# Gate and up of a feed-forward layer: weights stationary against tokens stationary, with the results turned by block transposes and DMAs

## The chip, the cores and the metric

One core of a Trainium2 chip runs the whole kernel. The metric is device time in microseconds (us), the median of several runs. PE is the tensor engine (matmul), PEld its weight load, DVE the vector engine, ACT the scalar engine, POOL the engine for general work, SP the one that issues most DMAs. All arithmetic is in float32; each big product is made of three passes of a split form (below).

## The reference, cut to what matters

Two transformer blocks, 256 tokens (S) by 2048 features (D), batch 1. The first has a sliding-window attention; the second has two attention branches and a gated feed-forward layer. What the change touches is the end of the second block:

```python
h2 = rmsnorm_2(x, ffn_norm_g[i])
x = x + (jax.nn.silu(h2 @ w_ffn_gate[i]) * (h2 @ w_ffn_up[i])) @ w_ffn_down[i]
return rmsnorm_2(x, final_norm_g)
```

`w_ffn_gate` and `w_ffn_up` are 2048 x 5632, `w_ffn_down` is 5632 x 2048.

## The kernel before

**Split form.** A matrix entry is held as hi + lo, hi rounded to the matmul's format and lo the rest. A product is hi x hi + hi x lo + lo x hi. Weights come from HBM in chunks of 16 tiles of 128 x 128 (1 MB, by SP, four buffers); `Weights.cut` (line 60) splits half a chunk (8 tiles) at a time: ACT casts to w_hi (line 84), DVE subtracts to w_lo (line 85). Four halves of each are held, so the splits run up to four halves ahead of PE and then wait for PE to give a buffer back.

**Two forms of product.** `gemm` (line 319) keeps a weight tile stationary and moves the tokens: per tile one 512-column matmul (hi weights against hi and lo of the 256 tokens side by side) and one 256-column matmul (lo weights against hi tokens); `runs` (line 307) does eight of one kind, then eight of the other. Its result has features on partitions and tokens along the row. `gemm_nat` (line 375) with `nat3` (line 367) keeps a 128 x 128 block of tokens stationary and moves four weight tiles (512 columns): hi x hi, hi x lo, lo x hi, for each of two token blocks, so six 512-column matmuls per row of four weight tiles. Its result has tokens on partitions.

**The stage.** After the product `out`, x2 holds the residual and `h` the 16 normed blocks (features on partitions, h3_0 to h3_15). Gate and up are `gemm` products, 44 blocks of 128 columns each: for each block m the gate product, its scaling by the norm's factor (a row broadcast `rb` made by `rows`, line 282, with a matmul), Silu, the up product, the multiply, and a split into `act[m]`, which has features on partitions as the down product needs it. The first four products run together over four banks (`gemm4`, line 329). The down product is `gemm_nat`, tokens stationary; its results are added to x2n, the residual turned to tokens on partitions.

**What sets the order.** `between` (line 126) holds generators of side work. Every product calls `between.tiles`, and after `between.every` weight tiles (16 here) one step of side work is written into the program; `yield n` asks for n such ticks of pause. In this stage the side work is `after_out` (line 940): it makes the norm's factor r_3, the broadcast, and then eight x2n pieces, each from four PE transposes and a copy on ACT. A scheduler orders the instructions of each engine from that program; every engine runs its own list in order. POOL computes the norms' powers (line 279) and issues five DMAs: a table (`lam`) and the four gain tiles `fgt` (line 978). Small tiles come from one pool, `unit`, of 67 buffers of 128 x 512.

Of the kernel before, what the change touches and what calls it, by code (L numbers as in the profile page):

```python
# [9 lines left out]
F32 = mybir.dt.float32  # L10
# [4 lines left out]
P = 128  # L15
S = 256
# [154 lines left out]
def block_kernel(ctx, tc, order, w, x01, xt, bc, fg, cst, out):  # L171
# [10 lines left out]
    def unit(name, dt=F32):  # L182
        return up.tile([P, 512], dt, name=name, tag="u", bufs=NU)
# [4 lines left out]
    def bank(tag):  # L188
        return psum.tile([P, 512], F32, name=f"ps_{tag}", tag=tag, bufs={"g": 4, "s": 2, "t": 2}[tag])
# [92 lines left out]
    def rows(r, rb=None):  # L282

        dg = unit("diag")[:, 0:S]
        for tb in range(2):
            nc.vector.tensor_scalar(out=dg[:, tb * P:tb * P + P], in0=ident, scalar1=r[:, tb:tb + 1], scalar2=None,
                                    op0=ALU.mult)
        ps = bank("t")
        mm(ps[:, 0:S], ones, dg, True, True)
        if rb is not None:  # L290
            nc.vector.tensor_copy(out=rb, in_=ps[:, 0:S])
        return ps[:, 0:S]
# [73 lines left out]

    def nat3(o, hl, tb, hi, lo, first, last):

        xh = hl[:, tb * P:tb * P + P]
        xl = hl[:, S + tb * P:S + tb * P + P]  # L370
        mm(o, xh, hi, first, False)
        mm(o, xh, lo, False, False)
        mm(o, xl, hi, False, last)
# [13 lines left out]
    def total(o, ps):  # L387

        nc.scalar.copy(out=o, in_=ps[:, S:])  # L389
        tt(o, o, ps[:, 0:S], ALU.add)  # L390

    def scaled(o, ps, rb):
        total(o, ps)
        tt(o, o, rb, ALU.mult)
# [24 lines left out]
    def transposed(p, on_act=False):  # L419

        ps = bank("t")
        for j in range(3):
            nc.tensor.transpose(out=ps[:, j * P:j * P + P], in_=p[:, j * P:j * P + P], identity=ident)  # L423
        pt = unit("prob_t")[:, 0:384]
        if on_act:
            nc.scalar.copy(out=pt, in_=ps[:, 0:384])
        else:
            nc.vector.tensor_copy(out=pt, in_=ps[:, 0:384])
        return pt


    sq = Squares(8)
# [493 lines left out]
    for m, ps in blocks("out", 0, 16, mg):  # L926
# [5 lines left out]
        split_scaled(t, gcol(G_FFN, m), hl)  # L932
        h.append(hl)
        sq.add(t)
    rb = unit("rb_3")[:, 0:S]
    r_3 = const.tile([P, 2], F32, name="r_3")
    x2n = []

    def after_out():
        yield  # L940
        nc.vector.tensor_copy(out=r_3, in_=rstd(sq.sums(), D))
        yield
        rows(r_3, rb)
        for cb in range(4):
            for tb in range(2):
                yield
                ps = bank("t")
                for i in range(4):
                    nc.tensor.transpose(out=ps[:, i * P:i * P + P], in_=x2[4 * cb + i][:, tb * P:tb * P + P],  # L949
                                        identity=ident)  # L950
                t = unit("x2n")
                nc.scalar.copy(out=t, in_=ps)
                x2n.append(t)

    between.every, between.apart = 16, 1
    between.add(after_out())
    act = []
    for m in range(0, KF):
        if m == 0:
            b4 = gemm4("ffn", [0, KF, 1, KF + 1], h)  # L960
        t = unit("ffn")
        zg, zu = t[:, 0:S], t[:, S:]
        ps = b4[2 * m] if m < 2 else gemm("ffn", m, h)
        scaled(zg, ps, rb)
        nc.scalar.activation(out=zg, in_=zg, func=AF.Silu)
        ps = b4[2 * m + 1] if m < 2 else gemm("ffn", KF + m, h)
        total(zu, ps)
        tt(zu, zu, zg, ALU.mult)
        hl = unit(f"act{m}", F32R)
        split_scaled(zu, None, hl)  # L970
        act.append(hl)
    between.drain()

    tot = sm("tot", 10)
    fgt = []
# [81 lines left out]
    return c  # L1057


def _columns(v):  # L1060
    return np.asarray(v, np.float32).reshape(-1, P).T


def _matrices(i):

    pairs = []
    for j in range(16):
        kt = j // 8
        for hd in (16 * kt + j % 8, 16 * kt + 8 + j % 8):
            pairs.extend(range(hd * 64, hd * 64 + 64))  # L1070
    pairs = np.array(pairs)
    in_a, in_2 = i["w_in_a"][0], i["w_in_2"][0]
    uq = i["w_uq_2"][0].reshape(768, 16, 192)
    ukv = i["w_ukv_2"][0].reshape(512, 16, 256)
    kpe = in_2[:, 1280:1344]
    ffn = np.concatenate([i["w_ffn_gate_2"][0], i["w_ffn_up_2"][0]], axis=1)
    return {
        "in_a": np.concatenate([in_a[:, :2048][:, pairs], in_a[:, 2048:2560], in_a[:, 2560:][:, pairs]], axis=1),
        "out_a": i["w_out_a"][0][pairs],
        "in_2": in_2[:, :1280],  # L1080
        "kpe": np.concatenate([kpe, kpe], axis=1),
        "dqk": in_2[:, 1344:5440],
        "dv": in_2[:, 5440:7488],
        "gate": in_2[:, 7488:],
        "uq": np.concatenate([uq[:, :, :128].reshape(768, -1), uq[:, :, 128:].reshape(768, -1)], axis=1),
        "uk": ukv[:, :, :128].reshape(512, -1),
        "uv": ukv[:, :, 128:].reshape(512, -1),
        "mla": i["w_mla_proj_2"][0],
        "diff": i["w_diff_proj_2"][0],
        "out": i["w_out_2"][0],  # L1090
        "ffn": ffn,
        "down": i["w_ffn_down_2"][0],
    }


# [32 lines left out]
```

## Time and profile before

| | us |
|---|---|
| median of 3 runs | 2023.06 (2022.99 to 2024.19) |
| profiled execution | 2023.11 |
| its span | 2021.3 |
| gate and up, first matmul to down's first | 494.40 |
| down, first matmul to its last part | 233.69 |

PE is busy 2007.7 us of the span, DVE 1309.4, ACT 1074.6, POOL 18.4; 364.83 MB move by DMA, 180 GB/s on average. The mean granted clock of PE is 0.999 of full speed. A matmul's own duration overlaps the next one's, so a pace is read from one start to the next. A table by stage gives for each engine its busy time and, in brackets, its instructions.

### The profile page before, as it was taken

To read this page: it belongs to the slowest core of one execution; us is meant where nothing else is said; L and a number is where in the kernel's file an instruction comes from. 1 tells how busy PE (TensorE), PEld (TensorE's weight loads), DVE (VectorE), ACT (ScalarE), POOL (GpSimd) and SP (SyncE) were. 2 spreads that over 40 slices of the span, in tenths; PEclk is the share of its full clock that TensorE was granted. 3 is DMA by queue.
4 is the path that set the end of the run, shared out by engine and by line. 5 is a ranking of instruction groups with operands and counts; after the bars stand their busy time and mean duration, and the time that the engine had idled before them with its cause. 6 is when DMAs were issued, how large, how long until landed. Compare 5 with 4: busy or idle time off the path is not lost.

```text
span 2021.3 us, 28390 instructions
## 1 busy us (share of the span) xinstructions
PE 2007.7 (99%) x11338; PEld 1744.3 (86%) x11338; DVE 1309.4 (65%) x2151; ACT 1074.6 (53%) x1821; POOL 18.4 (1%) x25
## 2 busy tenths in 40 slices
PE   9999999999999999999999999999999999999998
PEld 8888888888888888888888888888888888888887
DVE  7778766887857555576665667656666666554544
ACT  6677665756546444455565445554444445444443
POOL 0000000000000000000000000000000000000000
PEclk9999999999999999999999999999999999999999
DMA  8444454444344555545445555455555555555553
GB/s 300 152 144 149 165 209 176 167 149 155 135 169 167 188 188 188 190 167 186 172 166 188 192 196 190 175 179 187 189 188 189 192 191 191 194 209 189 196 197 104
DMA packets 53235, 364.83 MB, mean 180 GB/s; under 512 B 6064, under 2 KB 6576, under 8 KB 9968
## 3 DMA queue, kind: packets, MB, share of 16 engines
q1 hardware_dynamic: 51552, 359.76, 49.8%
q10 hardware_dynamic: 1152, 1.97, 0.3%
q8 instruction: 88, 1.44, 0.3%
q0 software_dynamic: 400, 1.31, 0.2%
q14 instruction: 43, 0.35, 0.1%
HBM read 360.91 MB, written 2.10 MB: 180 GB/s over the span
## 4 chain that ended last, share of the span: by engine, by line
PE 96%; DVE 2%; ACT 1%; issue 1%; DMA 0%; POOL 0%; POOLq 0%; ACTq 0%
PE ps_g L198 88%; PE ps_s L198 5%; PE ps_t L198 2%; PE ps_t L423 1%; DVE rope_t L201 1%; DVE w_lo L85 0%; DVE k_n L201 0%; DVE q_r L201 0%; ACT w_hi L84 0%; DMA x01t<-x 0%; PE ps_t L949 0%; PE ps_t L853 0%; ACT prob L414 0%; PE ps_t L829 0%; DVE prob L408 0%
## 5 line engine op out<-in xcount | busy, mean ns | idle before, releaser
L85 DVE TENSOR_TENSOR w_lo<-w_raw,w_hi 128x1024 fp32r<-128x1024 f32 (+1 forms) x677 | 824.9, 1220 | 296.7 <-ACT w_hi L84 276.3
L84 ACT CAST w_hi<-w_raw 128x1024 fp32r<-128x1024 f32 (+1 forms) x677 | 708.2, 1047 | 352.9 <-PE ps_g L198 269.5
L198 PE MATMUL ps_g<-h,w_hi 128*128 128x512 f32 x3048 | 742.1, 392 | 0.1
L198 PEld LDWEIGHTS ps_g<-h,w_hi 128*128 128x128 f32 x3048 | 558.4, 188 | 111.2 <-issue 3.5
L198 PEld LDWEIGHTS ps_g<-h,w_lo 128*128 128x128 f32 x3048 | 392.1, 191 | 17.8 <-issue 3.2
L198 PE MATMUL ps_g<-h,w_lo 128*128 128x256 f32 x3048 | 404.0, 284 | 0.0
L198 PE MATMUL ps_g<-w_hi,act 128*128 128x512 f32 x688 | 212.1, 389 | 0.0
L198 PEld LDWEIGHTS ps_g<-w_hi,act 128*128 128x128 f32 x688 | 129.1, 188 | 26.9
L389 ACT COPY ffn<-ps_g 128x256 f32<-128x256 f32 x86 | 31.8, 373 | 200.6 <-PE ps_g L198 200.6
L198 PE MATMUL ps_g<-w_lo,act 128*128 128x512 f32 x344 | 133.8, 389 | 0.0
L201 DVE TENSOR_TENSOR ffn<-ffn,ps_g 128x256 f32<-128x256 f32 x86 | 35.8, 420 | 143.9 <-ACT ffn L389 143.9
L198 PE MATMUL ps_g<-w_hi,h 128*128 128x512 f32 x256 | 79.5, 389 | 0.0
L198 PEld LDWEIGHTS ps_g<-w_lo,act 128*128 128x128 f32 x344 | 64.6, 188 | 13.3
L198 PE MATMUL ps_g<-y_m,w_hi 128*128 128x512 f32 x256 | 63.8, 391 | 0.0
L198 PE MATMUL ps_g<-y_d,w_hi 128*128 128x512 f32 x256 | 61.2, 391 | 0.0
L198 PE MATMUL ps_g<-g,w_hi 128*128 128x512 f32 (+1 forms) x240 | 57.8, 377 | 0.0
L198 PEld LDWEIGHTS ps_g<-w_hi,h 128*128 128x128 f32 x256 | 48.0, 188 | 10.0
L198 PE MATMUL ps_g<-mg,w_hi 128*128 128x512 f32 x224 | 56.0, 391 | 0.0
L198 PEld LDWEIGHTS ps_g<-y_m,w_hi 128*128 128x128 f32 x256 | 47.0, 188 | 9.1
L198 PEld LDWEIGHTS ps_g<-y_d,w_hi 128*128 128x128 f32 x256 | 47.0, 188 | 9.1
L198 PE MATMUL ps_g<-c,w_hi 128*128 128x512 f32 x208 | 53.0, 397 | 0.0
L198 PE MATMUL ps_g<-w_lo,h 128*128 128x512 f32 x128 | 49.8, 389 | 0.0
(255 smaller groups left out, 1899.4 us busy)
## 6 DMA issues: line engine op xcount, KB each, us to landing
w_raw<-w SPq DMA_DIRECT2D x337, 1024.0 KB, 4.8
w_raw<-w SPq DMA_DIRECT2D x5, 512.0 KB, 7.6
x_t<-xt SPq DMA_DIRECT2D x7, 256.0 KB, 7.4
fgt<-fg POOLq DMA_DIRECT2D x4, 256.0 KB, 5.5
out<-x2n SPq DMA_DIRECT2D x4, 256.0 KB, 3.1
out<-x2n ACTq DMA_DIRECT2D x4, 256.0 KB, 3.5
x01t<-x SPq DMA_DIRECT2D x1, 310.0 KB, 4.8
w_raw<-w ACTq DMA_DIRECT2D x1, 256.0 KB, 5.0
```

What stands on the lines that cost most here:

```text
L84: a = nc.scalar.copy(out=hi[:, q], in_=src[:, q])
L85: b = nc.vector.tensor_tensor(out=lo[:, q], in0=src[:, q], in1=hi.bitcast(F32)[:, q], op=ALU.subtract)
L198: nc.tensor.matmul(out=o, lhsT=a, rhs=b, start=start, stop=stop, skip_group_check=True)
L201: nc.vector.tensor_tensor(out=o, in0=a, in1=b, op=op)
L389: nc.scalar.copy(out=o, in_=ps[:, S:])
L423: nc.tensor.transpose(out=ps[:, j * P:j * P + P], in_=p[:, j * P:j * P + P], identity=ident)
```

## The change

Gate and up become `gemm_nat` products, 11 groups of four blocks: one gate product of 512 columns, one up product of 512 columns, each for two token blocks. The norm's factor is now a scalar per partition inside Silu, so the broadcast goes (and, as before, the up half is left unscaled until the end). The result has tokens on partitions and has to be turned. DVE transposes 32 x 32 blocks in place within a 128 x 512 tile (`nc.vector.transpose`); then `moved` exchanges the blocks between partition quarters with 16 DMAs of 32 partitions x 128 columns, issued by POOL. `split_act`, added to `between` after each group, waits five ticks and then splits the two pieces into act_hi and act_lo. The x2n pieces are turned the same way, with no PE transposes: the first three ticks after r_3, the others eight ticks apart. The columns of gate, up, down, the final gain and the output are permuted on the host (`_quarters`) so that the blocks come out in place. `between.drain()` ahead of the down product is gone: the last group's split is written inside down's first product.

```diff
     def nat3(o, hl, tb, hi, lo, first, last):
-        xh = hl[:, tb * P:tb * P + P]
-        xl = hl[:, S + tb * P:S + tb * P + P]
+        if isinstance(hl, list):
+            xh, xl = hl[tb]
+        else:
+            ...
+    def moved(tr, name):
+        o = unit(name)
+        for a in range(4):
+            for b in range(4):
+                nc.gpsimd.dma_start(out=o[32 * b:32 * b + 32, a * P:a * P + P],
+                                    in_=tr[32 * a:32 * a + 32, b * P:b * P + P])
+        return o
     def after_out():
         yield
         nc.vector.tensor_copy(out=r_3, in_=rstd(sq.sums(), D))
-        yield
-        rows(r_3, rb)
         for cb in range(4):
             for tb in range(2):
-                yield
-                ps = bank("t")
+                yield 8 if x2n else 3
+                tr = unit("x2_t")
                 for i in range(4):
-                    nc.tensor.transpose(out=ps[:, i * P:i * P + P], in_=x2[4 * cb + i][:, tb * P:tb * P + P],
-                                        identity=ident)
-                t = unit("x2n")
-                nc.scalar.copy(out=t, in_=ps)
-                x2n.append(t)
+                    nc.vector.transpose(
+                        out=tr.rearrange("p (a m j) -> p a m j", a=4, m=4)[:, :, i, :],
+                        in_=x2[4 * cb + i][:, tb * P:tb * P + P].rearrange("p (a j) -> p a j", a=4))
+                x2n.append(moved(tr, "x2n"))
-    for m in range(0, KF):
-        if m == 0:
-            b4 = gemm4("ffn", [0, KF, 1, KF + 1], h)
-        t = unit("ffn")
-        zg, zu = t[:, 0:S], t[:, S:]
-        ps = b4[2 * m] if m < 2 else gemm("ffn", m, h)
-        scaled(zg, ps, rb)
-        nc.scalar.activation(out=zg, in_=zg, func=AF.Silu)
-        ps = b4[2 * m + 1] if m < 2 else gemm("ffn", KF + m, h)
-        total(zu, ps)
-        tt(zu, zu, zg, ALU.mult)
-        hl = unit(f"act{m}", F32R)
-        split_scaled(zu, None, hl)
-        act.append(hl)
-    between.drain()
+    def split_act(u, parts):
+        yield 5
+        hls = []
+        for t in parts:
+            t = t.rearrange("p (a g i) -> p g a i", a=4, g=4)
+            hi, lo = unit("act_hi", F32R), unit("act_lo", F32R)
+            nc.scalar.copy(out=hi.rearrange("p (g a i) -> p g a i", a=4, g=4), in_=t)
+            tt(lo.rearrange("p (g a i) -> p g a i", a=4, g=4), t,
+               hi.bitcast(F32).rearrange("p (g a i) -> p g a i", a=4, g=4), ALU.subtract)
+            hls.append((hi, lo))
+        for k in range(4):
+            q = slice(k * P, k * P + P)
+            act[4 * u + k] = [(hi[:, q], lo[:, q]) for hi, lo in hls]
+    for u in range(KF // 4):
+        parts = []
+        for tb, ps in enumerate(gemm_nat("ffn", u * 512, h)):
+            z = unit("ffn")
+            nc.scalar.activation(out=z, in_=ps, func=AF.Silu, scale=r_3[:, tb:tb + 1])
+            parts.append(z)
+        for tb, ps in enumerate(gemm_nat("ffn", DFF + u * 512, h)):
+            z = parts[tb]
+            tt(z, ps, z, ALU.mult)
+            tr = unit("ffn_t")
+            nc.vector.transpose(out=tr, in_=z)
+            parts[tb] = moved(tr, "ffn_m")
+        between.add(split_act(u, parts))
```

How the instructions stand, at three places. First PE, inside one of the early up products of before: the end of the lo passes of a product (bank ps_g_12681, normed blocks h3), four transposes of residual tiles y into ps_t, and the next hi passes.

```order
L198 MATMUL ps_g_12681<-h3_14_12241,w_lo_12689 128x256
L198 MATMUL ps_g_12681<-h3_15_12292,w_lo_12689 128x256
L949 MATMUL ps_t_12716<-ident_117,y_2855 128x128 x2
L949 MATMUL ps_t_12716<-ident_117,y_2856 128x128 x2
L198 MATMUL ps_g_12681<-h3_8_11935,w_hi_12688 128x512
L198 MATMUL ps_g_12681<-h3_9_11986,w_hi_12688 128x512
```

The same engine after the change, the first row of weights of the third group's gate product and the start of the next: two banks, one per token block, and every matmul 512 columns wide.

```order
L198 MATMUL ps_g_12999<-w_hi_13003,h3_0_11657 128x512
L198 MATMUL ps_g_12999<-w_lo_13004,h3_0_11657 128x512
L198 MATMUL ps_g_12999<-w_hi_13003,h3_0_11657 128x512
L198 MATMUL ps_g_13000<-w_hi_13003,h3_0_11657 128x512
L198 MATMUL ps_g_13000<-w_lo_13004,h3_0_11657 128x512
L198 MATMUL ps_g_13000<-w_hi_13003,h3_0_11657 128x512
L198 MATMUL ps_g_12999<-w_hi_13003,h3_1_11664 128x512
```

The short lo passes and the transposes are gone from PE; hi, lo, hi alternate, so a half's w_lo is wanted one matmul after its w_hi.

Second ACT, which splits the weights ahead of PE. Before, block 10: between the casts stand the copy of a product's second part, Silu, and the cast of the result.

```order
L389 COPY ffn_13340<-ps_g_13341 128x256
L84 CAST w_hi_13445<-w_raw_13439 128x1024
L965 ACTIVATE ffn_13340<-ffn_13340 128x256
L84 CAST w_hi_13488<-w_raw_13486 128x1024
L389 COPY ffn_13340<-ps_g_13388 128x256
L84 CAST w_hi_13492<-w_raw_13486 128x1024
L234 CAST act10_13434<-ffn_13340 128x256
```

After, in the third group's up product: three of its eight halves are cast, then the Silu of the third group's gate, the fourth half, and then the casts of the second group's two pieces (ffn_m_12962 and the next) with the fifth half between.

```order
L84 CAST w_hi_13161<-w_raw_13143 128x1024
L84 CAST w_hi_13201<-w_raw_13199 128x1024
L986 ACTIVATE ffn_13137<-ps_g_12999,r_3_12298 128x512
L986 ACTIVATE ffn_13139<-ps_g_13000,r_3_12298 128x512
L84 CAST w_hi_13217<-w_raw_13199 128x1024
L973 CAST act_hi_13233<-ffn_m_12962 128x512
L84 CAST w_hi_13243<-w_raw_13241 128x1024
L973 CAST act_hi_13237<-ffn_m_12982 128x512
L84 CAST w_hi_13259<-w_raw_13241 128x1024
```

The casts of a piece stand 12 and 13 halves behind the end of the product that made it, in front of later halves of weights; the last group's stand together, 11 halves into the down product. DVE's list has the same pattern with w_lo and act_lo.

Third POOL. Before, nothing stands between the factor of the norm and the four gain tiles.

```order
L279 TENSOR_TENSOR rstd_12393<-ms_12391,mhalf_115 128x2
L978 DMA fgt_16639<-fg 128x512
L978 DMA fgt_16641<-fg 128x512
L978 DMA fgt_16643<-fg 128x512
L978 DMA fgt_16645<-fg 128x512
L1022 TENSOR_TENSOR rstd_18160<-ms_3_18127,mhalf_115 128x1
```

After, with the waits shown: the end of the 16 DMAs of the second group's second piece, and the start of the 16 of a residual piece.

```order
L439 DMA ffn_m_12982<-ffn_t_12980 32x128 [waits DMASW6_49]
L439 DMA ffn_m_12982<-ffn_t_12980 32x128 [waits DMASW7_49]
L439 DMA ffn_m_12982<-ffn_t_12980 32x128 [waits DMASW0_49]
L439 DMA x2n_13182<-x2_t_13177 32x128 [waits DMASW1_49,DVE_49,Activation_49]
L439 DMA x2n_13182<-x2_t_13177 32x128 [waits DMASW2_49]
L439 DMA x2n_13182<-x2_t_13177 32x128 [waits DMASW3_49]
```

480 such DMAs now stand between the norm's factor and the gain tiles; eight semaphores (DMASW0 to DMASW7) go round, and each DMA waits for the one eight places earlier.

## Rows read from the trace of the kernel before

**Rows 1.** The page: busy time of PE, granted clock by slice, the chain

```profile
PE 2007.7 (99%) x11338; PEld 1744.3 (86%) x11338; DVE 1309.4 (65%) x2151; ACT 1074.6 (53%) x1821; POOL 18.4 (1%) x25
...
PEclk9999999999999999999999999999999999999999
...
PE 96%; DVE 2%; ACT 1%; issue 1%; DMA 0%; POOL 0%; POOLq 0%; ACTq 0%
```

**Rows 2.** By stage: length, then busy us of PE, PEld, DVE, ACT, POOL

```profile
1278.91:1773.31 494.40, 494.40 (x2855) 437.17 (x2854) 303.82 (x398) 249.07 (x357) 2.87 (x5) 1.00 0.53 188
1773.31:2007.00 233.69, 233.69 (x1032) 193.51 (x1031) 115.29 (x109) 95.20 (x103) 0.00 (x0) 1.00 0.51 182
```

**Rows 3.** Timeline of PE in gate and up: start, length, instructions merged

```profile
1359.54 3.82 PE L198 MATMUL ps_g<-h,w_hi 128*128 128x512 f32 x16
...
1365.10 3.82 PE L198 MATMUL ps_g<-h,w_hi 128*128 128x512 f32 x16
```

**Rows 4.** Timeline of PE in the down product

```profile
1990.00 0.62 PE L198 MATMUL ps_g<-w_hi,act 128*128 128x512 f32 x2
...
1990.68 0.62 PE L198 MATMUL ps_g<-w_hi,act 128*128 128x512 f32 x2
```

**Rows 5.** The chain in order of time, early gate and up: start, length

```profile
1312.96 5.57 PE ps_g L198 x32
1318.53 0.44 PE ps_t L949 x4
1318.97 5.57 PE ps_g L198 x32
```

**Rows 6.** Timeline: sums and broadcast on PE, h3_15 and r_3 on DVE

```profile
1281.39 0.48 DVE L238 SCALAR_TENSOR_TENSOR h<-y,x01t,h 128x256 fp32r<-128x256 f32 x1
...
1290.08 0.50 PE L198 MATMUL ps_t<-ones,sq 128*128 128x1 f32 x4
...
1290.99 0.63 PE L198 MATMUL ps_s<-h,w_hi 128*128 128x512 f32 x2
...
1291.65 0.17 DVE L941 COPY r<-rstd 128x2 f32<-128x2 f32 x1 [0.87 <-POOL rstd L279]
...
1295.66 0.62 PE L198 MATMUL ps_s<-h,w_hi 128*128 128x512 f32 x2
1296.12 0.59 PE L198 MATMUL ps_t<-diag,ones 128*128 128x256 f32 x2
...
1297.02 0.62 PE L198 MATMUL ps_s<-h,w_hi 128*128 128x512 f32 x2
```

**Rows 7.** Groups and tiles: busy and mean ns, or ns min/median/max

```profile
L85 DVE TENSOR_TENSOR w_lo<-w_raw,w_hi 128x1024 fp32r<-128x1024 f32 x153 | 187.4, 1225 | 26.2 <-ACT w_hi L84 20.1
L84 ACT CAST w_hi<-w_raw 128x1024 fp32r<-128x1024 f32 x153 | 161.1, 1053 | 19.1 <-PE ps_g L198 9.6 <-ACT w_hi L84 0.5
...
L983 DVE SCALAR_TENSOR_TENSOR x2n<-ps_g,r,x2n x7: 741/744/750, 1832.9 to 2007.4; 128x512 f32<-128x512 f32 x7
L201 DVE TENSOR_TENSOR x2n<-x2n,fgt x6: 684/685/686, 1835.6 to 1955.9; 128x512 f32<-128x512 f32 x6
...
L880 ACT ACTIVATE v_hi<-ps_g,r x8: 690/690/690, 608.8 to 1005.5; 128x512 fp32r<-128x512 f32 x8
```

**Rows 8.** POOL's DMAs (issue, landing) and powers; DVE beside the gain tiles

```profile
L978 POOL DMA_DIRECT2D fgt<-fg x4: 538/538/581, 1771.0 to 1772.6; - x4
...
L566 POOL DMA_DIRECT2D lam<-bc x1: 702/702/702, 97.4 to 97.4; - x1
...
fgt<-fg POOLq DMA_DIRECT2D x4, 256.0 KB, 5.5
...
lam<-bc POOLq DMA_DIRECT2D x1, 256.0 KB, 3.1
...
L279 POOL TENSOR_TENSOR rstd<-ms,mhalf x14: 690/697/1613, 38.6 to 1290.9; 128x2 f32<-128x2 f32 x14
...
1770.84 1.23 DVE L85 TENSOR_TENSOR w_lo<-w_raw,w_hi 128x1024 fp32r<-128x1024 f32 x1 [0.58 <-ACT w_hi L84]
```

More of the change, by code (lines that the diff above doesn't have):

```diff
@@ L367, in nat3 @@
     def nat3(o, hl, tb, hi, lo, first, last):
-        xh = hl[:, tb * P:tb * P + P]
-        xl = hl[:, S + tb * P:S + tb * P + P]
+        if isinstance(hl, list):
+            xh, xl = hl[tb]
+        else:
+            xh = hl[:, tb * P:tb * P + P]
+            xl = hl[:, S + tb * P:S + tb * P + P]
         mm(o, xh, hi, first, False)
@@ L934, in block_kernel @@
         sq.add(t)
-    rb = unit("rb_3")[:, 0:S]
     r_3 = const.tile([P, 2], F32, name="r_3")
@@ L955, in block_kernel @@
+                x2n.append(moved(tr, "x2n"))
     between.every, between.apart = 16, 1
     between.add(after_out())
-    act = []
-    for m in range(0, KF):
-        if m == 0:
-            b4 = gemm4("ffn", [0, KF, 1, KF + 1], h)
-        t = unit("ffn")
-        zg, zu = t[:, 0:S], t[:, S:]
-        ps = b4[2 * m] if m < 2 else gemm("ffn", m, h)
-        scaled(zg, ps, rb)
-        nc.scalar.activation(out=zg, in_=zg, func=AF.Silu)
-        ps = b4[2 * m + 1] if m < 2 else gemm("ffn", KF + m, h)
-        total(zu, ps)
-        tt(zu, zu, zg, ALU.mult)
-        hl = unit(f"act{m}", F32R)
-        split_scaled(zu, None, hl)
-        act.append(hl)
@@ L972, in block_kernel @@
-    between.drain()
+    act = [None] * KF
+    def split_act(u, parts):
[11 more added lines that the diff above has]
+            act[4 * u + k] = [(hi[:, q], lo[:, q]) for hi, lo in hls]
@@ L1057, in _constants, with _quarters @@
     return c
+def _quarters(n):
+    return np.arange(n).reshape(-1, 4, 4, 32).transpose(0, 2, 1, 3).reshape(-1)
 def _columns(v):
@@ L1075, in _matrices @@
     kpe = in_2[:, 1280:1344]
-    ffn = np.concatenate([i["w_ffn_gate_2"][0], i["w_ffn_up_2"][0]], axis=1)
+    ffn = np.concatenate([i["w_ffn_gate_2"][0], i["w_ffn_up_2"][0]], axis=1)[:, _quarters(2 * DFF)]
     return {
@@ L1091, in _matrices @@
         "ffn": ffn,
-        "down": i["w_ffn_down_2"][0],
+        "down": i["w_ffn_down_2"][0][:, _quarters(D)],
     }
@@ L1109 @@
             "sinks_a", "lambda_q1_2", "lambda_q2_2", "lambda_k1_2", "lambda_k2_2")])[None], (P, 1)),
-        "fg": np.tile(i["final_norm_g_2"].reshape(1, D), (P, 1)),
+        "fg": np.tile(i["final_norm_g_2"][_quarters(D)].reshape(1, D), (P, 1)),
         "cst": _constants(),
@@ L1126 @@
     res = _run(nc, [arrays], core_ids=[0])
-    return res.results[0]["out"].reshape(1, S, D)
+    out = np.empty((1, S, D), np.float32)
+    out[0][:, _quarters(D)] = res.results[0]["out"].reshape(S, D)
+    return out
```

## The prediction

> **What bounds the kernel now.** I read the page first: the busy lines, the slices and the chain. TensorE (PE) is busy 99% of the span, its granted clock stands at full speed in every slice, and PE matmuls are 96% of the chain that ended last [rows 1]. So no other engine is late for long, and what an edit is worth is what it takes from, or adds to, PE's stream of matmuls. Next the table by stage [rows 2]: gate and up run from 1278.91 to 1773.31 (494.40 us), the down product from 1773.31 to 2007.00 (233.69 us), both with PE busy throughout. In gate and up VectorE (DVE) is busy 303.82 of 494.40 us and ScalarE (ACT) 249.07, so both have room.
>
> Mean durations of matmuls overlap their neighbours, so the pace must be read from start to start. In gate and up, one product (16 weight tiles, each a 512-column hi pass and a 256-column lo pass) starts at 1359.54 and the next at 1365.10: 5.56 us, or 0.3475 us per weight tile [rows 3]. In the down product the tokens are stationary already; there the groups "w_hi x2, w_lo" (three 512-column matmuls) start at 1990.00 and 1990.68: 0.680 us for three, 0.2267 us each [rows 4]. A row of weights (four tiles wide) takes six of them, 1.360 us, or 0.340 us per tile. The whole down stage confirms this pace: 168 rows at 1.360 are 228.5 us, 8 more for one token block alone 5.4 us, together 233.9 against 233.69.
>
> **The change, part by part.**
>
> *Products.* Gate and up have 2 x 44 x 16 = 1408 weight tiles. Before: 88 products x 5.56 = 489.3 us. After: 22 products (11 gate, 11 up) of 16 weight rows, 352 x 1.360 = 478.7 us. The columns streamed are the same (768 per tile); six long matmuls replace four long and four short ones, and each matmul costs a few cycles beyond its columns. Gain 10.6 us, all on PE, so all on the path.
>
> *Transposes that leave PE.* Before, 32 PE transposes of the residual lie between the products, four in each of eight places, 0.44 us a place, and the product beside them takes 6.01 us from start to start (1312.96 to 1318.97) where the steady one takes 5.56 [rows 5]: 8 x 0.45 = 3.6 us. The row broadcast of the norm's factor (one diag matmul) pushes the stream from 0.93 us for four matmuls to 1.36 (1295.66 to 1297.02) [rows 6]: 0.4 us. Both go. The four small sums matmuls stay.
>
> *Sum on PE.* Parts: 10.6 + 3.6 + 0.4 = 14.6 us. By the ends of the stage: 494.4 before; after, 478.7 plus 0.45 for the sums (1290.08 to 1290.99, 0.91 us where two matmuls take 0.46) is 479.2; gain 15.2 us [rows 2, 6]. The 0.6 between them is the first product of before, run over four banks, which I did not split further. I take the ends: **15.2 us**.
>
> *DVE and ACT per group of four blocks* (one gate and one up product, 43.5 us of PE time). DVE: 16 weight splits x 1.225 = 19.6; two gate-times-up multiplies from PSUM, about the 0.744 of the residual's op on the same tile size: 1.5; two act_lo subtractions at 0.685: 1.4; two block transposes and four of residual pieces a quarter as wide, which the trace does not show: at the same 0.744 for a full width 2.2, at twice that 4.5. Sum 25 to 27 of 43.5. ACT: 16 x 1.053 = 16.8, two Silu and two casts at the 0.690 of the v_hi op: 19.6 of 43.5 [rows 7]. Costed at nothing: PE's stream hides them.
>
> *POOL's DMAs, the unknown.* Each group's two results, after the transposes, are moved by 16 DMAs each, 32 x 512 B; so are the eight residual pieces, one per group for eight groups: 480 DMAs, up to 48 in a group, all on one queue. In the order each DMA waits for the eighth before it, so a DMA costs the larger of its issue and an eighth of its landing. Nothing of this shape stands in the trace; the nearest rows are the gain tiles (four DMAs of 256 KB, issued in 0.54 to 0.58 us each, landing in 5.5) and one table (0.70, landing in 3.1) [rows 8]. A landing of 5.5 over eight is 0.69. So I bound a DMA at 0.54 to 0.70 us and take 0.60; these are smaller (16 KB), which speaks for the low end. A group's 48 then take 26 to 34 us of 43.5: the queue keeps up.
>
> *The wait it adds.* act_hi on ACT and act_lo on DVE wait for all 16 DMAs of a piece; queued behind them are the weight splits, for which PE waits. Call the end of a group's up product T. DVE then does two multiplies and one transpose, so the DMAs start near T + 2.2. The last of 32 lands at T + 2.2 + 32 x 0.60 + 3.1 = T + 24.5 (T + 22.6 at 0.54; T + 30.1 at 0.70 and 5.5). In the order the first act_hi stands after the 12th half chunk of weights past T, the second after the 13th; a half (8 tiles) lasts PE 2.72 us, so the 14th is wanted at T + 35.4. Ahead of it lie cast 0.69, subtraction 0.69 and split 1.22 = 2.6 us. Deadline T + 32.8: met, with 2.7 us to spare even at the upper bounds. The last group is tighter: both act_hi stand after the 11th half, so the 12th, wanted at T + 29.9, sets the deadline T + 27.3. At 0.60 it holds by 2.8 us; at the upper bounds it is missed by 2.8, once. I take 0 and keep 2.8 for the range. The pieces themselves are needed only at the 41st row of the down product, T + 54.4.
>
> *Moved past.* The gain tiles' four DMAs now stand on POOL behind the last 32: they issue by about T + 25 and are wanted after the first down product, T + 60, so nothing. The factor r_3 is wanted by the first Silu, 21.8 us into the stage; before, it was ready 12.9 us in. The last of the 16 normed blocks is wanted at the 16th weight row, 20.4 us in, and is split within the first 3.0 [rows 6]. SP's weight loads keep their order: 1 MB per 5.44 us in place of 5.56.
>
> **A rule against it.** Beside the gain tiles' DMAs DVE was splitting weights (1770.84 to 1772.07) and their issue times stayed at 538 to 581 ns [rows 8]. The Trainium skill, page "SBUF — State Buffer", section "SBUF: two separate sides", warns that a DMA issued from GpSimd can be starved of descriptors while DVE holds the shared port, and gives some 620 ns alone against 3100 beside a copy; by that figure, as an estimate, the 48 DMAs of a group would fill 149 us instead of 43.5 and the change would lose far over 500 us. That rule is rival 1 at its strongest; the row does not show it beside weight splits, and what block transposes do no row here tells.
>
> **Rivals.**
>
> 1. *POOL's queue becomes the bound* (slower). For: some POOL instructions are stretched already, the norm factor's power takes 0.69 us in most places and 1.61 in others, with DVE at work beside it; eight DMAs of small pieces wait on landings. Against: the 538 to 581 ns above. Priced at half of that stretch on each DMA, 0.54 + 0.46 = 1.0 us [rows 8]: seven groups of 48 us instead of 43.5 add 31.5; the last three groups have only 32 DMAs but their second piece lands at T + 39.7, late by 6.9, 6.9 and 12.4: 26.2. 2007.9 + 57.7 = **2065.6**. It decides from where 11 groups' lateness eats 15.2 us: with ten deadlines of 32.8 and one of 27.3, that is 0.81 us a DMA with landing in 5.5, 0.89 with 3.1.
> 2. *The queue keeps up, but the pieces land a little late*: 0.80 us a DMA and a landing of 5.5 put the last at T + 33.3, 0.5 us late in ten groups and 6.0 in the last: 11.0 lost, **2018.9**. For: the deadlines are fixed places in ACT's order. Against: it needs a DMA slower than any row.
> 3. *It does not gain what it says*: with hi, lo, hi in turn, the lo half of a chunk is wanted right after its hi half, where before eight hi passes lay between. If DVE's split then sets the pace, the stage stays near 494 and the time near **2023**. Against: the down product runs this pattern at 0.2267 us with no gap [rows 4].
>
> **How the numbers follow.** The profiled execution took 2023.11 us, its span 2021.3, 1.8 us outside; the median of the three runs is 2023.06, so the two agree. 2023.1 - 15.2 = **2007.9**. Chances: forecast 0.82 (2006.5 to 2011: 14.6 to 15.2 gained, up to 2.8 given back, half a microsecond of spread), rival 2 0.07, rival 1 0.08, rival 3 0.03. The forecast's own range holds 0.82 but leaves no room for a mis-sized landing; I reach into rival 2: 2006.0 to 2015.0. Within 0.2% (4 us; about what a measurement can tell from no change) lies rival 3 and a part of 2: faster 0.87, same 0.05, slower 0.08.
>
> **What would show it.** Right: down's first matmul near 1758 instead of 1773.3; "w_hi x2, w_lo" groups 0.680 us apart through gate and up; act_hi hardly waiting; POOL's DMAs starting under 0.7 us apart. Wrong: ACT's waits on software DMAs at act_hi with w_hi late behind them and PE idle once a group (rivals 1 and 2); PE groups further apart than 0.68 with waits on w_lo (rival 3). A DMA above 0.85 us would overturn the sign.

## The result and the profile after

The changed kernel takes **2012.2 us** (median, 2012.12 to 2012.29) where the kernel before takes 2023.03 beside it: a ratio of 0.9945, 95% interval 0.9928 to 0.9963. That is a gain of 10.8 us, or 0.5%; I had forecast 15.2 us. The profiled execution of after took 2012.29 us with a span of 2010.4.

The table by stage is the place to begin, because the forecast was a sum over stages. Columns as in [rows 2]: length, then busy us of PE, PEld, DVE, ACT and POOL with instruction counts, granted clock, DMA share, GB/s. First the kernel after: gate and up, the down product up to its last part, and the end of the program.

```profile
1278.64:1757.86 479.22, 479.22 (x2117) 396.84 (x2116) 259.24 (x275) 211.79 (x221) 220.04 (x449) 1.00 0.60 209
1757.86:1991.60 233.74, 233.74 (x1033) 193.55 (x1032) 115.98 (x107) 94.17 (x99) 17.81 (x36) 1.00 0.52 184
1991.60:2010.40 18.80, 6.09 (x50) 5.85 (x48) 4.40 (x10) 4.42 (x10) 1.12 (x2) 0.79 0.34 113
```

The same last stretch of the kernel before (its first two stages are [rows 2]):

```profile
2007.00:2021.30 14.30, 6.14 (x50) 5.89 (x48) 4.40 (x10) 4.41 (x10) 1.12 (x2) 0.85 0.44 147
```

Gate and up went from 494.40 to 479.22 us, a gain of 15.18; down is the same within 0.05. But the end is 4.50 us longer, with the same instructions in it and the same busy times on PE, DVE, ACT and POOL to 0.05 us. So what the stage gained, less what the end lost, is the result: 15.2 - 4.5 = 10.7. Nothing that the busy times count got longer at the end; something there waits.

Neither the page nor the chain names it. The chain's last pieces in order of time (start, length, what) have the same steps as in before, and no long one behind the last work:

```profile
1994.34 4.66 issue
1998.99 0.60 POOLq L1144
1999.60 0.02 issue
1999.62 1.33 ACT x2n L1053 x2
```

The chain ends at 2000.95, the span at 2010.40. What lies between are instructions that the views leave out: the program's closing steps, which the trace records all the same. Here are those of POOL and SP (start, length in ns, engine, instruction). First of before:

```
  2014.44   1084 GpSimd  DRAIN
  2014.48    554 GpSimd  TENSOR_TENSOR
  2020.47      7 Sync    DRAIN
  2020.53      7 Sync    DRAIN
  2020.56     17 GpSimd  EVENT_SEMAPHORE
```

and of after:

```
  1998.99  10644 GpSimd  DRAIN
  1999.04    552 GpSimd  TENSOR_TENSOR
  2005.39      7 Sync    DRAIN
  2005.46      7 Sync    DRAIN
  2009.69     17 GpSimd  EVENT_SEMAPHORE
```

All engines meet at a semaphore that POOL hands on (the EVENT_SEMAPHORE row). In before POOL's drain, which begins beside the last power, takes 1.08 us and is long done when SP has seen the last output land (2020.53). In after it takes 10.64 us; SP is ready at 2005.46 and POOL only at 2009.69. Those 4.2 us are most of the 4.50. The other 0.3 come ahead of SP's last step (13.86 us from the start of this stretch, 13.53 in before); the cause of these is not shown. The question for the experiments is what makes POOL's drain ten times as long.

The rest of the profile after, for the steps of the prediction. PE's stream in gate and up (timeline; start, length, instructions), which answers [rows 3] and [rows 4]: "w_hi x2, w_lo" starts every 0.68 us.

```profile
1499.91 0.62 PE L198 MATMUL ps_g<-w_hi,h 128*128 128x512 f32 x2
1500.37 0.39 PE L198 MATMUL ps_g<-w_lo,h 128*128 128x512 f32 x1
1500.60 0.62 PE L198 MATMUL ps_g<-w_hi,h 128*128 128x512 f32 x2
```

POOL's moves and the transposes (by tile: ns minimum/median/maximum, first and last start), and the time from a move's issue to its landing:

```profile
L439 POOL DMA_DIRECT2D ffn_m<-ffn_t x352: 496/496/501, 1324.9 to 1780.1; - x176
...
DMA to landing us min/median/max: 1.6/4.1/6.7
```

```profile
L992 DVE STREAM_TRANSPOSE ffn_t<-ffn x22: 699/701/703, 1323.6 to 1760.5; 128x512 f32<-128x512 f32 x22
...
L958 DVE STREAM_TRANSPOSE x_t<-y x32: 267/268/306, 1300.6 to 1605.9; 128x128 f32<-128x128 f32 x32
```

One group's 32 moves on POOL, timeline with the idle time before each piece and what ended it, and DVE beside their start:

```profile
1368.33 4.40 POOL L439 DMA_DIRECT2D ffn_m<-ffn_t  x9 [13.57 <-ACT w_hi L84]
1373.64 0.50 POOL L439 DMA_DIRECT2D ffn_m<-ffn_t  x1 [0.90 <-DMA ffn_m<-ffn_t]
1374.82 3.92 POOL L439 DMA_DIRECT2D ffn_m<-ffn_t  x8 [0.69 <-DMA ffn_m<-ffn_t]
1379.48 3.91 POOL L439 DMA_DIRECT2D ffn_m<-ffn_t  x8 [0.75 <-DMA ffn_m<-ffn_t]
1383.91 0.50 POOL L439 DMA_DIRECT2D ffn_m<-ffn_t  x1 [0.51 <-DMA ffn_m<-ffn_t]
1385.15 2.44 POOL L439 DMA_DIRECT2D ffn_m<-ffn_t  x5 [0.74 <-DMA ffn_m<-ffn_t]
```

```profile
1367.71 1.19 DVE L85 TENSOR_TENSOR w_lo<-w_raw,w_hi 128x1024 fp32r<-128x1024 f32 x1
1368.82 0.70 DVE L992 STREAM_TRANSPOSE ffn_t<-ffn 128x512 f32<-128x512 f32 x1
```

32 moves run from 1368.33 to 1387.59: 19.3 us, or 0.60 each, with runs of mostly eight or nine issued back to back and then a wait for the landing of the eighth before. Over the eleven groups it is 0.60 to 0.65 each, and 0.71 in the third, where a long pause falls (see "The residual turned on PE"). They start 0.49 apart also while DVE transposes (1368.82 to 1369.52 lies inside the first nine).

### The profile page after: what moved, and what is told of

It is laid out like the page before. It is cut to its first block, busy times and chain, and to the rows that moved or that the text cites. A ratio compares the mean times of both kernels' runs of the same rounds, so it can differ in the third digit from the quotient of the medians.

```text
span 2010.4 us, 27424 instructions
## 1 busy us (share of the span) xinstructions
PE 1991.8 (99%) x10600; PEld 1703.7 (85%) x10600; DVE 1265.3 (63%) x2026; ACT 1036.5 (52%) x1681; POOL 253.4 (13%) x505
## 4 chain that ended last, share of the span: by engine, by line
PE 96%; DVE 2%; ACT 1%; issue 1%; DMA 0%; POOL 0%; POOLq 0%; SPq 0%; ACTq 0%
PE ps_g L198 89%; PE ps_s L198 4%; PE ps_t L198 2%; PE ps_t L426 1%; DVE rope_t L201 1%; DVE w_lo L85 0%; DVE k_n L201 0%; DVE q_r L201 0%; DMA w_raw<-w 0%; ACT w_hi L84 0%; PE ps_t L865 0%; ACT prob L417 0%; PE ps_t L841 0%; DVE prob L411 0%; DVE y_m L235 0%
## 5 line engine op out<-in xcount | busy, mean ns | idle before, releaser
L198 PE MATMUL ps_g<-w_hi,h 128*128 128x512 f32 x1664 | 513.5, 389 | 0.0
L198 PE MATMUL ps_g<-h,w_hi 128*128 128x512 f32 x1672 | 410.3, 393 | 0.6 <-DVE h L238 0.6
L198 PEld LDWEIGHTS ps_g<-w_hi,h 128*128 128x128 f32 x1664 | 312.3, 188 | 64.9
L198 PEld LDWEIGHTS ps_g<-h,w_hi 128*128 128x128 f32 x1672 | 306.2, 188 | 63.1 <-issue 3.5
L198 PE MATMUL ps_g<-w_lo,h 128*128 128x512 f32 x832 | 323.7, 389 | 0.0
L198 PE MATMUL ps_g<-h,w_lo 128*128 128x256 f32 x1672 | 223.1, 284 | 0.0
L198 PEld LDWEIGHTS ps_g<-h,w_lo 128*128 128x128 f32 x1672 | 214.3, 191 | 10.4 <-issue 3.2
L439 POOL DMA_DIRECT2D ffn_m<-ffn_t x352 | 172.3, 497 | 222.8 <-ACT w_hi L84 86.1
L198 PEld LDWEIGHTS ps_g<-w_lo,h 128*128 128x128 f32 x832 | 156.2, 188 | 32.4
L198 PE MATMUL ps_g<-w_hi,act_hi 128*128 128x512 f32 x344 | 133.8, 389 | 0.0
```

What stands on the lines that cost most here:

```text
L198: nc.tensor.matmul(out=o, lhsT=a, rhs=b, start=start, stop=stop, skip_group_check=True)
L439: nc.gpsimd.dma_start(out=o[32 * b:32 * b + 32, a * P:a * P + P], in_=tr[32 * a:32 * a + 32, b * P:b * P + P])
```

## The experiments

**Theories.** A: POOL's closing drain costs about 20 ns for each DMA that POOL has issued and no drain has settled yet, (10.64 - 1.08) / 480. B: the long drain has another cause at the program's end and the number of DMAs has nothing to do with it. C came up after the first four runs: the drain costs by what is still unsettled in POOL's queue, and the queue settles itself now and then.

### A drain ahead of time

```diff
         nc.gpsimd.dma_start(out=t, in_=fg[:, cb * 512:cb * 512 + 512])
         fgt.append(t)
+    pin(nc.gpsimd.drain())
```

> The changed kernel with one more instruction: a drain of POOL right behind its four gain tiles' DMAs, in the down product, where POOL has nothing to do for some 210 us. Theory A: POOL's closing drain takes about 20 ns for each DMA that POOL has queued and that no drain has settled yet (1.08 us behind 5 DMAs before, 10.64 behind 485 after, so 9.56 / 480), and the program's end waits for it. Then the added drain takes some 10 us beside the down product, the closing one about 1.1 us, the span ends 0.7 us behind SP's last step instead of 4.9, and the time is 2012.2 - 4.2 = 2008.0. Theory B: the long drain comes from something else at the program's end (POOL's longer program being fetched, the wait for the two small powers): it stays near 10.6 us and the time at 2012.2.

Measured: **2008.14 us** (2007.8 to 2009.13), ratio to before 0.9924 (0.9907 to 0.994). The records of POOL and SP:

```
  1783.18  10611 GpSimd  DRAIN
  1999.18    668 GpSimd  DRAIN
  1999.22    553 GpSimd  TENSOR_TENSOR
  2005.59      7 Sync    DRAIN
  2005.66      7 Sync    DRAIN
  2005.69     17 GpSimd  EVENT_SEMAPHORE
```

The 10.6 us moved into the down product, where POOL has nothing to do, and the closing drain is 0.67. The three stages of this kernel, as in the first table:

```profile
1278.82:1758.05 479.23, 479.23 (x2117) 396.84 (x2116) 259.22 (x275) 211.70 (x221) 219.88 (x449) 1.00 0.60 209
1758.05:1991.79 233.74, 233.74 (x1033) 193.55 (x1032) 115.96 (x107) 94.18 (x99) 17.79 (x36) 1.00 0.52 185
1991.79:2006.40 14.61, 6.09 (x50) 5.85 (x48) 4.41 (x10) 4.42 (x10) 1.12 (x2) 0.80 0.44 145
```

Only the last stretch differs from after: 14.61 instead of 18.80. Theory B falls: with the same program but for one instruction, the drain at the end is short. The 0.3 us by which this stretch is longer than the 14.30 of before stay, so they are not the drain's. The kernel is faster than after and before, and its 2008.14 us lie 0.2 above the 2007.9 that I had forecast for the change.

### The kernel before with 480 more DMAs

```diff
     for m in range(0, KF):
+        for j in range(11 if m < 40 else 10):
+            q = 128 * (j % 4)
+            nc.gpsimd.dma_start(out=junk[j:j + 1, q:q + 128], in_=ones[j:j + 1, :])
```

> The kernel before with 480 more DMAs on POOL and nothing else of the change: each moves one row of 128 columns (512 B) of a constant tile to a tile that nothing reads. Theory A, counted by DMAs: the closing drain grows from 1.08 to 10.6 us, about 6.1 of it lie beside SP's last waits, and the time is 2023.0 + 4.3 = 2027.3, with gate, up and down as before. Theory A, counted by the rows that the DMAs move (480 x 32 in the change, here 480 x 1): the drain grows by 0.3 us and the time stays 2023.0. Theory B: 2023.0.

Measured: 2060.23 us, 33 above what theory A had said. The time is no test, because the DMAs depend on nothing and were put at the start of POOL's list: they run until 288 us, and the first norm's power and the table `lam` stand among them (60.60 and 174.22 us instead of 38.60 and 97.37). PE's waits (us in total, times, longest):

```profile
PE ps_t L198 <- DVE diag L286: 16.8, 2, 16.2
PE ps_t L423 <- ACT o_a L524: 11.0, 1, 11.0
```

I had not thought of where they would land. The end is a test all the same: gate and up take 494.40 us as before, and POOL's drain takes 10.637 us, with the span ending 5.3 us behind SP's last drain where in before it is 0.8. So 480 DMAs alone, in a kernel without transposes or token-stationary gate and up, make the long drain, and one row a DMA does it as well as 32: neither bytes nor rows count.

### The residual turned on PE

```diff
-                tr = unit("x2_t")
-                for i in range(4):
-                    nc.vector.transpose(...)
-                x2n.append(moved(tr, "x2n"))
+                ps = bank("t")
+                for i in range(4):
+                    nc.tensor.transpose(out=ps[:, i * P:i * P + P], in_=x2[4 * cb + i][:, tb * P:tb * P + P],
+                                        identity=ident)
+                t = unit("x2n")
+                nc.scalar.copy(out=t.rearrange("p (a m j) -> p m a j", a=4, m=4),
+                               in_=ps.rearrange("p (m a j) -> p m a j", m=4, a=4))
+                x2n.append(t)
```

> The changed kernel with the eight residual pieces turned as before, by four PE transposes each and a copy on ACT; 352 of the 480 DMAs stay. The prediction's step: the transposes cost PE 3.6 us, so the down product starts at 1761.5 instead of 1757.9. Theory A: the closing drain is 1.08 + 352 x 0.0199 = 8.1 us instead of 10.6, so 2.5 come back at the end: 2012.2 + 3.6 - 2.5 = 2013.3. Theory B: nothing comes back, 2015.8.

Measured: 2015.73 us (2015.63 to 2016.97). The stage is 3.87 us longer than in after, 0.48 a piece where the prediction had 0.45:

```profile
1279.75:1762.84 483.09, 483.09 (x2149) 400.06 (x2148) 252.92 (x243) 215.62 (x229) 157.24 (x321) 1.00 0.58 203
```

But the drain is 10.07 us, not 8.1: with 128 DMAs fewer it lost 0.57 us. The time came out at what theory B had said, for neither B's reason nor A's. A, in which each DMA counts the same, falls here too.

What led on was POOL's timeline. In after there is one long pause in the middle of a piece, at the 129th DMA, that is put down to a split of DVE's with which a move has nothing to do:

```profile
1418.12 2.45 POOL L439 DMA_DIRECT2D ffn_m<-ffn_t  x5 [0.82 <-DMA ffn_m<-ffn_t]
1423.23 3.97 POOL L439 DMA_DIRECT2D ffn_m<-ffn_t  x8 [2.66 <-DVE w_lo L85]
```

From start to start 3.16 us pass there, where the steps beside it take 0.49; the same pause stands at the 250th and the 371st DMA (3.10 us at 1526.55, 3.12 at 1641.47), so every 121. So theory C: the queue holds 128 entries; when it is full POOL stops and settles the 121 that have landed, and a drain pays for what has come since. With 7 entries left over at each such stop, after ends with 485 - 370 + 7 = 122 unsettled entries, x2n_on_pe with 357 - 249 + 7 = 115. With 0.67 us behind none (the closing drain above) and 1.08 behind 5 (before), that is 0.082 us an entry in all four.

### Twelve DMAs more, and four

```diff
         fgt.append(t)
+    junk = const.tile([P, 512], F32, name="junk")
+    for j in range(12):
+        nc.gpsimd.dma_start(out=junk[j:j + 1, 0:P], in_=ones[j:j + 1, :])
```

(and `range(4)`). If C holds, adding DMAs must make the kernel faster once the count passes 491.

> The changed kernel with 12 more DMAs on POOL behind the four gain tiles, each one row of 512 B to a tile that nothing reads: 497 in all instead of 485. Theory C: POOL's queue holds 128 entries; when it is full POOL pauses (3.1 us in the trace of after, at the 129th, 250th and 371st DMA, so every 121, with 7 entries still there) and settles what has landed, and a drain takes 0.67 us plus 0.082 for each entry that is still unsettled (0.67 behind none, 1.08 behind 5, 10.07 behind 115 where 357 DMAs ran, 10.64 behind 122 where 485 did). The 492nd DMA then brings the next pause, in the down product where nothing waits, 13 entries are left, the closing drain is 1.7 us and the time 2008.0: more DMAs, shorter. Theory A (20 ns for each DMA since the start): drain 10.9, time 2012.5.

> As plus_12 with 4 more DMAs instead of 12, 489 in all. Theory C: no further pause, 126 entries, closing drain 0.67 + 126 x 0.082 = 11.0 us, time 2012.6. Theory A: 10.7, 2012.3. Together with plus_12 it shows whether the drain falls when the count passes 491.

Measured: with 12 more **2008.66 us** (2008.53 to 2008.91; ratio to before 0.9928, 0.9913 to 0.9943), closing drain 1.742 us; with 4 more 2012.47 in one run on the same chip, closing drain 10.972 us. With 12 the pause came at the 492nd DMA, the last but one of the moves, in the down product (POOL's timeline):

```profile
1777.38 1.96 POOL L439 DMA_DIRECT2D ffn_m<-ffn_t  x4 [0.73 <-DMA ffn_m<-ffn_t]
1782.05 0.98 POOL L439 DMA_DIRECT2D ffn_m<-ffn_t  x2 [2.72 <-issue]
```

(The order put the extra DMAs in different places, so it is a move that stands behind the pause.) POOL's closing drains in four kernels, of plus_12, plus_4, x2n_on_pe and before_480 in this order:

```
  1999.56   1742 GpSimd  DRAIN
  1998.81  10972 GpSimd  DRAIN
  2003.97  10072 GpSimd  DRAIN
  2047.09  10637 GpSimd  DRAIN
```

All drains together, each against 0.668 + 0.0818 x entries:

| kernel | DMAs | entries since the last pause, + 7 | drain, us | by the line |
|---|---|---|---|---|
| drain_early, closing | 485 | 0 | 0.668 | 0.668 |
| before | 5 | 5 (no pause) | 1.084 | 1.077 |
| plus_12 | 497 | 13 | 1.742 | 1.731 |
| x2n_on_pe | 357 | 115 | 10.072 | 10.075 |
| halved_moves (below) | 965 | 118 | 10.319 | 10.320 |
| after | 485 | 122 | 10.644 | 10.648 |
| before_480 | 485 | 122 | 10.637 | 10.648 |
| plus_4 | 489 | 126 | 10.972 | 10.975 |

The line has two constants fitted, and the 7; it then holds to 0.011 us in all eight (the drain added in drain_early, which begins beside the last gain tiles, is 0.04 below it), and it said beforehand that 497 would be short and 489 long. That the drain grows with the DMAs since the last pause or drain, and not with all of them, is what the runs show; that these are entries of a ring of 128 which wait to be settled is my reading of the 129th and of the 121. One thing does not fit a single price: the pause takes about 2.6 us more than an ordinary step (3.1 against 0.49) for 121 entries, the drain 10 us for as many. Why the drain is the dearer of the two no run shows.

### What a move costs the queue

```diff
     for a in range(4):
         for b in range(4):
-            nc.gpsimd.dma_start(out=o[32 * b:32 * b + 32, a * P:a * P + P],
-                                in_=tr[32 * a:32 * a + 32, b * P:b * P + P])
+            for i in (0, 16):
+                nc.gpsimd.dma_start(out=o[32 * b + i:32 * b + i + 16, a * P:a * P + P],
+                                    in_=tr[32 * a + i:32 * a + i + 16, b * P:b * P + P])
```

> The changed kernel with each move made by two DMAs of 16 rows instead of one of 32: 960 DMAs, the same rows and bytes. It asks what a move costs POOL's queue. If a DMA costs 0.50 to 0.60 us whatever it moves (issue 0.497, an eighth of a landing of 4.1), a group's 96 take 48 to 58 us of 43.5 while the residual pieces run: the queue falls behind by 4.5 to 14 us a group for eight groups. The order puts the casts of the pieces up to 13 halves later than in the changed kernel, which covers the first figure and not the second: 2012 at 0.50, about 2080 at 0.60, with POOL without a pause between groups. If the cost goes with the rows, the 96 take 29 us and the time stays 2012. By rival 1 of the prediction PE then waits for w_hi behind a cast of a piece.

Measured: 2101.94 us in one run. From one DMA to the next it is 0.60 us while the queue is busy (0.59 to 0.66 over successive windows of 96), half the rows or not. So 960 need some 576 us, more than the 479 of the stage, and the stage takes 561.7. What waits is what the prediction's rival 1 said: ACT at the cast of a piece, with w_hi queued behind it, then PE (waits in gate and up: us in total, times, longest).

```profile
ACT act_hi L974 <- DMA ffn_m<-ffn_t: 158.6, 16, 15.8
```

```profile
PE ps_g L198 <- ACT w_hi L84: 47.1, 10, 11.0
PE ps_g L198 <- DVE w_lo L85: 11.1, 13, 1.6
```

It came out 22 us above the 2080 that I had put beside 0.60 us; PE stands for 58 us of the 82.5 that the stage grew. The other 24 are work: PE is busy 503.4 us instead of 479.2, at a mean granted clock of 0.95 (see the last section).

### The products alone, everything turned on PE

```diff
+            ps = bank("t")
+            for k in range(4):
+                nc.tensor.transpose(out=ps[:, k * P:k * P + P], in_=t[:, k * P:k * P + P], identity=ident)
             hi, lo = unit("act_hi", F32R), unit("act_lo", F32R)
-            nc.scalar.copy(out=hi.rearrange("p (g a i) -> p g a i", a=4, g=4), in_=t)
+            nc.scalar.copy(out=hi, in_=ps)
...
-            tr = unit("ffn_t")
-            nc.vector.transpose(out=tr, in_=z)
-            parts[tb] = moved(tr, "ffn_m")
```

(The residual pieces are turned as in the kernel before, and the columns keep their order.)

> The products of the change alone: gate and up with the tokens stationary, but the results and the residual are turned by PE transposes, four a piece (22 + 8 pieces), split from the bank that they fill; no block transposes, no moves, no permuted columns. By the prediction's steps the stage is 479.2 + 30 x 0.45 = 492.7 us; with 5 DMAs on POOL the closing drain is 1.1 and the end as short as before: 2008.0 + 13.5 = 2021.5. If the tokens-stationary products were not faster by themselves it would be above 2032; if PE's transposes were free beside them, 2008.

Measured: 2022.7 us (2022.08 to 2023.36), ratio to before 0.9997 (0.9988 to 1.0007). The time is 1.2 us above the 2021.5 expected; the stage and POOL's closing drain (1.086 us) are as expected:

```profile
1279.71:1772.47 492.76, 492.76 (x2230) 407.90 (x2228) 241.70 (x223) 214.78 (x229) 2.89 (x5) 1.00 0.54 190
```

28 of the 30 pieces lie in it: (492.76 - 479.22) / 28 = 0.48 us each, the same as for the residual's above; the last two lie in the down product and add 1.0 there. That the stage came out to 0.1 us is luck: 28 pieces at 0.48 make the same sum as the 30 at 0.45 that I had reckoned. So the products by themselves gain what was forecast, and 22 pieces more on PE give nearly all of it back. The moves off PE are what the change earns its time with.

### The moves from another queue

```diff
-                nc.gpsimd.dma_start(out=o[32 * b:32 * b + 32, a * P:a * P + P],
+                nc.sync.dma_start(out=o[32 * b:32 * b + 32, a * P:a * P + P],
```

(and `nc.scalar`). Both keep POOL's drain at 1.08 us.

> The changed kernel with the 480 moves issued by SP instead of POOL, in SP's list between the weight loads. Theory A: POOL has 5 DMAs again, its drain is 1.1 us and the end 4.2 us shorter: 2008.0, if no weight load comes late (16 moves at the 0.33 us that SP's output DMAs take are 5.3 us, and the loads run up to four chunks of 5.44 us ahead). Rival: the moves wait on SP for DVE's transposes with the weight loads queued behind them, PE then waits for w_hi, and the time is above 2012.2. Theory B leaves the end as it is: 2012.2 at best.

> The changed kernel with the 480 moves issued by ACT instead of POOL. POOL has 5 DMAs, its closing drain is 1.1 us. In the order 32 moves of a group stand on ACT with no cast of weights between them, each behind the landing of an earlier one; at the 0.50 to 0.60 us that a move took on POOL they hold ACT 16 to 19 us, and PE has at most four halves (10.9 us) split ahead. If so PE waits 5 to 8 us a group for w_hi: 2008 + 11 x (5 to 8) = 2063 to 2096. If ACT's moves went at its 0.34 us issue (the output DMAs) without waits, 32 take 10.9 us, all covered: 2008.

Measured: 2098.73 us from SP (2094.93 to 2100.59), 2223.87 from ACT in one run. On either queue 32 moves in a row take no less than on POOL, 0.65 to 0.71 us each, though they land in 1.8 us (median) instead of 4.1 (why, no run shows); and on these queues something urgent is behind them. SP's list in moves_on_sp, then ACT's in moves_on_act (timelines):

```profile
1373.40 20.84 SPq L439 DMA_DIRECT2D ffn_m<-ffn_t  x32
1394.34 0.53 SPq L53 DMA_DIRECT2D w_raw<-w  x1
```

```profile
1392.42 20.84 ACTq L439 DMA_DIRECT2D ffn_m<-ffn_t  x32
1413.35 3.89 ACT L84 CAST w_hi<-w_raw 128x1024 fp32r<-128x1024 f32 x4 [21.32 <-DMA ffn_m<-ffn_t]
```

From SP the weight loads come late: in gate and up ACT waits 108.1 us for w_raw, PE 45.7 us for w_hi.

```profile
ACT w_hi L84 <- DMA w_raw<-w: 108.1, 29, 9.0
```

From ACT the casts of the weights stand still for 21 us, twice what the four halves ahead (10.9 us) can cover.

```profile
PE ps_g L198 <- ACT w_hi L84: 164.9, 19, 14.4
```

My 0.50 to 0.60 us had the mechanism and not the size. At each of the eleven groups PE waits 12.6 to 14.4 us, 145.5 in all, where I had 5 to 8; the residual's 16 moves stall ACT a second time in eight groups, and PE 2.2 to 2.6 us each, 19.4 in all. That leaves 51 us of the 2223.87 above 2008 plus the waits, most of it work at the lower clock (last section).

## Why the prediction held where it did, and where it failed

**The direction, the range and the mechanism on PE held; the size was 4.3 us too hopeful.** 2012.2 lies inside 2006.0 to 2015.0, above the forecast's own 2006.5 to 2011. That it lies inside the wider range is luck: I had reached up to 2015.0 for pieces that land late, which did not happen, and not for anything at the program's end.

- **Products, transposes, broadcast: 15.2 us forecast, 15.18 measured.** 478.7 + 0.45 gave 479.2 for the stage, and 479.22 came; down's first matmul stands at 1757.86 where I had written "near 1758". The split of the sum holds too: the pace is 0.680 us for three matmuls, and a piece of four PE transposes costs 0.48 between token-stationary products, where 0.45 was taken from [rows 5]. x2n_on_pe shows the parts: 494.40 - 483.09 = 11.31 us for products and broadcast, where the parts said 10.6 + 0.4, and 3.87 for the residual's pieces, where they said 3.6. (The broadcast is two matmuls in [rows 6], not one; its 0.4 us stand.)
- **DVE and ACT cost nothing.** DVE is busy 259.2 of 479.2 us, ACT 211.8, less than in before. A full-width block transpose takes 0.70 us, below the 0.744 that I had as the lower price; the 128 x 128 one 0.27.
- **POOL's queue: 0.60 us a DMA taken, 0.60 to 0.65 measured.** Issue is 0.50, lower than the bound of 0.54, and the wait for the eighth DMA before makes up the rest. By the prediction's own rule, the larger of the issue and an eighth of the landing, these rows would give 0.51 (4.1 / 8); the 0.60 was a middle between bounds from larger DMAs, so that it came so near is in part luck. That a landing takes 4.1 us and not 3.1 cost PE nothing.
- **The added wait: met, with less to spare than said.** For the last group the second cast of a piece started at T + 25.4 (T = 1757.86) against a deadline of T + 27.3; T + 24.5 had been the estimate. ACT waited once, for 4.58 us, and PE not at all:

```profile
1778.06 0.62 ACT L973 CAST act_hi<-ffn_m 128x512 fp32r<-128x512 f32 x1
1783.26 0.62 ACT L973 CAST act_hi<-ffn_m 128x512 fp32r<-128x512 f32 x1 [4.58 <-DMA ffn_m<-ffn_t]
```

- **The step that failed: "the sum is 2023.1 - 15.2".** It took everything behind the stage as unchanged. Every one of the 480 DMAs was priced where it is issued and where it lands, and none for what it leaves behind: the drain that closes the program pays 0.082 us for every one since POOL's last pause, which I read as entries that its queue keeps. 122 entries make 10.64 us, of which 6.5 lie beside SP's waits for the output (from 1998.99 to 2005.46) and 4.2 on the path. The prediction had put an edit's worth at what it takes from, or adds to, PE's stream, and had followed POOL's list only as far as the gain tiles; the drain closes the program and stands on neither. No row of before would have given the price, but its records did have a drain of 1.08 us on POOL and a closing step for which all engines meet.
- **The rule weighed.** POOL issues the 352 moves of results at 496 to 501 ns, with DVE transposing or splitting weights beside them (rows above), and the 128 of the residual at 496 to 544; in before it was 538 to 581 for larger ones [rows 8]. So the starvation of descriptors that the Trainium skill describes, page "SBUF — State Buffer", section "SBUF: two separate sides" (some 620 ns alone, 3100 beside a DVE copy), is not seen beside block transposes either. Those figures are for a copy, and no run here tells what a copy would do to the moves. The remedy of the Trainium skill, in the same section, is to issue such a DMA from the ACT or SP queue. Here that cost 86 us on SP and 212 on ACT against the changed kernel, because the moves held up work that PE waits for.
- **The rivals.** Rivals 2 and 3 did not happen. Rival 1's mechanism was shown when the moves were doubled (96 a group at 0.60 us where 72 fill the 43.5): ACT at act_hi, w_hi behind it, PE idle. Its price of 1.0 us a DMA was never near.

## What to carry to other kernels

Work that is taken off a busy engine and given to many small DMAs has two prices: the queue's time for each DMA, whatever its size, and, on POOL, what the queue still owes at the program's end. When a stage gains what was forecast and the whole does not, compare the stretch behind the last work in both traces, the closing drains too. If POOL issues hundreds of DMAs, drain it once in a stretch where it has nothing to do; that one instruction was worth 4 us here.

## What the runs showed of the hardware

- A drain of POOL takes 0.668 us plus 0.0818 us for each DMA issued on its queue since the last drain or pause (behind a pause, 7 more), long after all of them have landed (in after, POOL issued its last one at 1783.6, more than 200 us earlier). Rows and bytes do not matter: 1, 16 or 32 rows gave the same line. POOL pauses for some 3 us at the 129th DMA and every 121 after (2.7 to 3.4 us from start to start in the seven kernels that reach it, but for one of 5.0 in halved_moves), so the closing drain is a sawtooth in the number of DMAs, not a slope: 489 DMAs end with 10.97 us, 497 with 1.74.
- A DMA of 1, 16 or 32 rows of 512 B costs POOL about 0.60 us in a row: its price is one for each DMA. SP and ACT took 0.65 to 0.71 for 32 rows; other sizes were not tried there.
- PE's clock after a wait. In moves_on_act PE waited 12.63 us for w_hi (1401.8 to 1414.4). Stretches of 2 to 4 us, columns as in the first table, the granted clock being the third number from the end:

```profile
1400.00:1404.00 4.00, 1.82 (x9) 1.16 (x7) 0.00 (x0) 0.00 (x0) 0.00 (x0) 1.00 0.10 25
1404.00:1408.00 4.00, 0.00 (x0) 0.00 (x0) 0.00 (x0) 0.00 (x0) 0.00 (x0) 0.76 0.10 25
1408.00:1412.00 4.00, 0.00 (x0) 0.00 (x0) 0.00 (x0) 0.00 (x0) 0.00 (x0) 0.50 0.10 25
...
1416.00:1418.00 2.00, 2.00 (x5) 1.52 (x5) 2.00 (x3) 1.23 (x2) 0.00 (x0) 0.50 0.06 25
1418.00:1420.00 2.00, 2.00 (x7) 1.56 (x6) 1.06 (x1) 0.00 (x0) 0.00 (x0) 0.57 0.94 360
1420.00:1424.00 4.00, 4.00 (x19) 3.31 (x18) 1.25 (x2) 2.11 (x2) 0.00 (x0) 1.00 0.86 336
```

  During the wait the clock fell from full (2.4 GHz) to half (1.2 GHz), and PE ran at half for its first 5.3 us of work (until 1419.7): 5 matmuls in 2 us where 9 or 10 fit at full speed. So a wait of this length costs PE more than its length. In the stage of halved_moves PE worked 38.5 us while the trace's clock records stand at half; if work takes twice as long there, that makes some 19 of the 24 us beyond its waits, an estimate. The same estimate gives 21 of 29 us in moves_on_sp and 39 of 51 in moves_on_act. What the rest is, no run shows.
